# One hybrid decoder step: the small tile's own products cut in 32-column slices, meta updates over all 80 rows, and DeltaNet's sample keys and queries read as pairs

## The chip, the cores and the metric

The kernel runs on one NeuronCore of a Trainium2 chip. The metric is the time of the whole kernel on the device in microseconds (us), the median of several runs. One run was also recorded by the hardware profiler; rows called "the profile" or "the trace" come from that execution.

## The reference

One step of a decoder layer. A prompt of 1,024 tokens with 16 learned "meta" tokens in front, and 8 samples of 8 new tokens each, go through one input projection (2048 x 8984), three kinds of heads (6 mLSTM heads A, 6 gated-DeltaNet heads B, 4 HGRN2 heads C, each 128 wide), and an output projection (2048 x 2048). All values are 32-bit floats. For a prompt the state starts at zero and the 16 meta tokens are a chunk of their own; each sample starts from its own stored state.

```
# mLSTM, per chunk                    # gated DeltaNet, per chunk
num = a * (q @ C) + P @ v             W = U - Wk @ S
C_new = a_s * C + (w * k).T @ v       o = exp(G) * (q @ S) + Aqk @ W
n_new = a_s * n + sum(w * k)          S_new = exp(Ge) * S + (k * exp(Ge - G)).T @ W
# HGRN2, per chunk
o = (q * exp(b)) @ S + A @ v
S_new = exp(be) * S + (k * exp(be - b)).T @ v
```

So in each head every sample reads its own 128 x 128 state with its own 8 queries (DeltaNet with its 8 keys as well), while inside a sample, and among the 16 meta tokens, tokens see each other through a small masked matrix (P, Aqk, A).

## The kernel before, in words

The tokens are worked in two halves. Half 0 holds a **small tile** of 80 tokens (rows 0 to 63 are the 8 samples, 8 rows each; rows 64 to 79 are the meta tokens) and 512 prompt tokens in four tiles of 128. Half 1 holds the other 512 prompt tokens and no small tile. After both halves comes the output projection.

The bulk of the work on TensorE is the projection: a loop over weight pieces (`wraw`, loaded by SyncE's queue) that ScalarE and VectorE split into `whi` and `wlo`, multiplied with the tokens (`hA` in half 0, `hB` in half 1) into PSUM tiles `acc`. The heads' own work is written as generators and woven between these products: after each group of six `acc` products `weave.pump()` advances those head steps whose due time in a planner's clock has passed (each engine call adds a cost from a formula to that clock). The framework below may then move instructions on their engine. Every engine works through its own queue in order, so a TensorE product that waits holds back everything behind it there.

A 32-bit product stands in the trace as two instructions ("passes"). "128*32" in a row is rows times columns of TensorE's array that a product takes: rows are the partitions summed over, columns those of the result.

For the small tile in half 0 a head does this, and these are the places the change touches:

- `load_state` brings the 8 sample states of the head (512 KB) into `sst`, a single buffer.
- `sample_read` multiplies 8 samples' queries with their states: 8 products of 32 columns. Each sample's 8 columns stand in a zeroed block of 32 (`spread`), so that four samples add up in one group of 32 result rows and the read fills rows 0 to 63 of a PSUM tile: `nd` in A, `poh` in C, `po` in B. B calls it twice, for keys (`km`) and for queries (`qm`); the two `spread` tiles are used in turn by all heads.
- `small_rows` adds the tile's own products: one of 64 x 64 for the samples, one of 16 x 16 for the meta tokens.
- The meta tokens' state update is a product over the 16 meta rows alone (`pum` in A, `puh` in C, `pu` in B). In A a second product with `rowmask` over the 64 sample rows sums the keys for the normaliser `nsT`.
- In B, `side()` makes score matrices (`pqk`) and values (`pvb`) while VectorE inverts 16 x 16 blocks by substitution (`Yt`, `Yc` from coefficients `Bb` that went through memory); `px` transposes the result, and `first_chain` does the small tile's recurrence between the steps of the main tiles (`pz`, `pyy`, `px`).

Of the kernel before, what the change touches and what calls it, by code (L numbers as in the profile page):

```python
# [14 lines left out]
P = 128  # L15
# [165 lines left out]
def hybrid_step(ctx, tc, i, o):  # L181
# [353 lines left out]
    spread = [cp.tile([P, NB, 32], F32, name=f"spread{n}") for n in range(2)]  # L535
    spread_next = [0]
    for t in spread:
        G.memset(t, 0.0)

# [251 lines left out]
    def sample_read(st, src, dst, width, last=True):  # L791

        flat = src.rearrange("p b x -> p (b x)")
        for x in range(4):
            for j in range(2):
                b = 4 * j + x
                at_ = 32 * b - NS * x  # L800
                T.matmul(dst[32 * j:32 * (j + 1), 0:width], flat[:, at_:at_ + 32], st[:, b, 0:width],
                         start=x == 0, stop=last and x == 3)

    def small_rows(dst, rows, cols, width):

        for r in (slice(0, NSAMP), slice(NSAMP, NT0)):
            T.matmul(dst[r, 0:width], rows[r, r], cols[r, 0:width], start=r.start > 0, stop=True)
# [41 lines left out]
    def mlstm_scan(half, h, kT, qT, vT, tho, zs, nm, em, st):  # L849
# [52 lines left out]
        for g, kw, v1 in zip(half.groups, kws, v1s):  # L902
            if g.small:
                pu = bank("pum")
                T.matmul(pu[:, 0:P + 1], kw[NSAMP:NT0, 0], v1[NSAMP:NT0, 0], start=True, stop=True)
                T.matmul(pu[:, 2 * P:2 * P + NB], kw[0:NSAMP, 0], rowmask[0:NSAMP], start=True, stop=True)
                V.tensor_copy(Cn, pu[:, 0:P + 1])
                nsv = nsT.rearrange("p (b h) -> p b h", h=HA)[:, :, h:h + 1].rearrange("p b h -> p (b h)")
                nu = sp.tile([P, NB], F32, tag="nu", name="nu")
                V.tensor_tensor(nu, nsv, em[:, NS - 1:NSAMP:NS], op=ALU.mult)  # L910
                V.tensor_tensor(nsv, nu, pu[:, 2 * P:2 * P + NB], op=ALU.add)
                continue
# [16 lines left out]
        for g, E, kw, v1, og in zip(half.groups, Es, kws, v1s, ogs):  # L929
            n = g.n  # L930
            hx = gt("5", g)
            for c0 in range(0, g.nt, 2):
                cs = list(range(c0, min(c0 + 2, g.nt)))
                nd = bank("nd")
                for c in cs:
                    dst = nd[0:n, 256 * (c - c0):256 * (c - c0) + P + 1]
                    if g.small:
                        sample_read(st, qm, nd, P + 1, last=False)
                        small_rows(nd, E[:, c], v1[:, c], P + 1)
                        continue  # L940
                    T.matmul(dst, g.col(qd, c), Cn if c == 0 else Cs[:, c - 1], start=True, stop=False)
                    T.matmul(dst, E[0:n, c, 0:n], v1[0:n, c], start=False, stop=True)
# [80 lines left out]
    def gdn_scan(half, h, ck_, cq, cv, zs, Gb, eG, bb, st):  # L1023
# [70 lines left out]
        if half.first:  # L1094
            km, qm = spread_tile(), spread_tile()
            G.tensor_copy(km[:, :, 0:NS], sample_cols(knT))
            G.tensor_tensor(qm[:, :, 0:NS], sample_cols(cq), sample_cols(eG), op=ALU.mult)
# [31 lines left out]
        vbs, Aqs, kds = [], [], []  # L1129

        def side():
# [8 lines left out]
            yield  # L1140
            for g, kn in zip(gs, kns):
# [21 lines left out]
        def first_chain():  # L1163
            vb, Aq, kd, Y = vbs[0][:, 0], Aqs[0][:, 0], kds[0][:, 0], Ys[0][:, 0]
            po = bank("po0")
            sample_read(st, km, po, P)
# [8 lines left out]
            T.matmul(pu[:, 0:P], kd[NSAMP:NT0], W_[NSAMP:NT0], start=True, stop=True)  # L1175
            S.copy(Sm, pu[:, 0:P])
            po = bank("po1")
            sample_read(st, qm, po, P, last=False)
            small_rows(po, Aq, W_, P)
# [103 lines left out]
    def hgrn_scan(half, h, kT, lf, qT, vT, zs, st):  # L1283
# [90 lines left out]
        for g, v, kk in zip(gs, vs, kks):  # L1374
            pu = bank("puh")
            if g.small:
                T.matmul(pu[:, 0:P], kk[NSAMP:NT0, 0], v[NSAMP:NT0, 0], start=True, stop=True)
                V.tensor_copy(Sm, pu[:, 0:P])
                continue
# [10 lines left out]
        for g, v, kk in zip(gs, vs, kks):  # L1390
            n = g.n
            po = bank("poh")
            for c in range(g.nt):
                am = at0[0:n] if g.small else atv[:, c]
                dst = g.psum(po)[:, c]
                if g.small:
                    sample_read(st, qm, po, P, last=False)
                    small_rows(po, at0, v[:, 0], P)
                    continue
# [269 lines left out]
```

## Time and profile before

| | |
|---|---|
| median of 3 runs | 2603.36 us (2603.14 to 2606.81) |
| the profiled execution | 2607.68 us, span of its trace 2606.0 us |
| TensorE (PE) busy | 2549.4 us, 98% of the span |
| its weight loads (PEld), beside it | 2276.4 us, 87% |
| VectorE (DVE) | 1357.3 us, 52% |
| ScalarE (ACT) | 1005.8 us, 39% |
| GpSimd (POOL) | 533.6 us, 20% |
| memory | 121 GB/s over the span |

The profiled execution took 1.7 us more than its span. "Busy" joins instructions that overlap; a row of the timeline merges equal neighbours, so two products' lengths are compared by where rows start, not by the length printed. "[idle ... <- X]" at a row's end says how long the engine stood idle before it and what released it.

### The profile page before, as it was taken

The numbers are of one execution on the slowest core, as the hardware profiler recorded it, in microseconds if no ns is written. First come the engines' busy times: TensorE is split into PE (matmuls) and PEld (weight loads), VectorE is DVE, ScalarE is ACT, GpSimd is POOL, SyncE is SP. The second block draws the span as 40 slices with busy tenths as digits, with TensorE's granted clock in tenths as the row PEclk, the third lists the DMA queues.
The fourth block names the chain that finished last, engine by engine and source line by source line (L and its number), as shares of the span: only waits on it lengthen the run. The fifth ranks groups of instructions, "written<-read, shape, count | busy, mean of one in ns | idle before, by whom it ended". The sixth has DMA issues, their size and how long they took to land.

```text
span 2606.0 us, 43197 instructions
## 1 busy us (share of the span) xinstructions
PE 2549.4 (98%) x16160; PEld 2276.4 (87%) x16160; DVE 1357.3 (52%) x2811; ACT 1005.8 (39%) x2401; POOL 533.6 (20%) x656
## 2 busy tenths in 40 slices
PE   6899999999999999999999999999999999999998
PEld 5899999998999999999888888888888888888886
DVE  7664544654644654646674545455454545422435
ACT  5633334342334333324543434333433434322324
POOL 5221212321212321313230103111130102211201
PEclk9999999999999999999999999999999999999999
DMA  6633433555533433334644434343344437535735
GB/s 141 164 80 99 122 80 92 146 141 133 146 96 88 117 90 101 105 84 125 177 110 106 107 86 114 99 105 102 95 105 107 107 95 260 145 83 181 261 97 178
DMA packets 458461, 317.19 MB, mean 122 GB/s; under 512 B 56884, under 2 KB 402572, under 8 KB 457228
## 3 DMA queue, kind: packets, MB, share of 16 engines
q1 hardware_dynamic: 458252, 314.43, 44.6%
q8 instruction: 127, 2.08, 0.3%
q14 instruction: 82, 0.67, 0.1%
HBM read 268.93 MB, written 45.42 MB: 121 GB/s over the span
## 4 chain that ended last, share of the span: by engine, by line
PE 84%; issue 5%; DMA 4%; DVE 3%; POOL 2%; ACT 1%; SPq 1%; POOLq 0%; DVEq 0%; ACTq 0%
PE acc L127 60%; PE oacc L127 8%; PE pa L127 3%; PE po L127 1%; PE nd L127 1%; PE pu L127 1%; PE pz L127 1%; PE pyy L127 1%; POOL res L127 1%; PE poh L127 1%; DVE wlo L127 1%; POOL X L127 1%; PE pum L127 1%; PE py L127 1%; PE pw L127 0%
## 5 line engine op out<-in xcount | busy, mean ns | idle before, releaser
L127 PE MATMUL acc<-hA,whi 128*128 128x296 f32 x4544 | 837.8, 307 | 6.7 <-ACT whi L127 5.7
L127 DVE TENSOR_TENSOR wlo<-wraw,whi 128x512 fp32r<-128x512 f32 x720 | 520.9, 727 | 614.1 <-ACT whi L127 599.4
L127 ACT CAST whi<-wraw 128x512 fp32r<-128x512 f32 x720 | 443.3, 619 | 962.5 <-PE acc L127 667.0
L127 PE MATMUL acc<-hB,whi 128*128 128x512 f32 x2272 | 722.3, 400 | 0.0
L127 PEld LDWEIGHTS acc<-hA,whi 128*128 128x128 f32 x4544 | 683.1, 191 | 17.3 <-ACT whi L127 8.1
L127 PE MATMUL acc<-hA,wlo 128*128 128x296 f32 x2240 | 495.1, 301 | 5.3 <-DVE wlo L127 5.3
L127 PEld LDWEIGHTS acc<-hB,whi 128*128 128x128 f32 x2272 | 408.6, 188 | 76.6 <-issue 0.2
L127 PE MATMUL acc<-hB,wlo 128*128 128x512 f32 x1120 | 438.9, 392 | 1.2 <-DVE wlo L127 1.2
L127 PEld LDWEIGHTS acc<-hA,wlo 128*128 128x128 f32 x2240 | 368.0, 190 | 7.2 <-DVE wlo L127 6.9
L127 PE MATMUL oacc<-whi,y 128*128 128x512 f32 x1088 | 345.1, 392 | 1.4 <-ACT whi L127 1.4
L127 PEld LDWEIGHTS acc<-hB,wlo 128*128 128x128 f32 x1120 | 210.2, 188 | 48.9 <-DVE wlo L127 2.9
L127 PEld LDWEIGHTS oacc<-whi,y 128*128 128x128 f32 x1088 | 205.1, 189 | 45.1 <-ACT whi L127 2.7
L127 PE MATMUL oacc<-wlo,y 128*128 128x512 f32 x576 | 225.2, 391 | 0.7 <-DVE wlo L127 0.7
L127 PEld LDWEIGHTS oacc<-wlo,y 128*128 128x128 f32 x576 | 108.5, 188 | 23.8 <-DVE wlo L127 1.8
L127 POOL TENSOR_TENSOR res<-res,fnw 128x512 f32<-128x512 f32 (+1 forms) x34 | 54.3, 1623 | 259.1 <-ACT oscr L127 259.1
L127 POOL TENSOR_TENSOR qd<-qT,emb 128x512 f32<-128x512 f32 x12 | 15.9, 1326 | 359.1 <-PE po L127 287.2
L127 POOL TENSOR_TENSOR y<-y,zs 128x592 fp32r<-128x592 f32 (+1 forms) x32 | 45.9, 1434 | 140.3 <-ACT zs L127 130.1
L127 POOL TENSOR_TENSOR vx<-vh,rowmask 128x512 fp32r<-128x512 f32 x32 | 36.8, 1150 | 152.4 <-PE pu L127 79.5
L127 POOL TENSOR_TENSOR X<-Ex,hk 128x256 f32<-128x256 f32 (+2 forms) x40 | 37.4, 936 | 107.2 <-PE pa L127 93.0
L127 DVE TENSOR_TENSOR Yt<-Yc,Bb 128x60 f32<-128x60 f32 (+8 forms) x180 | 36.6, 203 | 43.7 <-DMA Bb<-db 38.6
L127 PE MATMUL pa<-X 128*128 128x128 f32 (+2 forms) x480 | 57.8, 260 | 0.0
L127 PEld LDWEIGHTS pa<-X 128*128 128x128 f32 (+2 forms) x480 | 50.0, 165 | 8.6 <-issue 0.9
(394 smaller groups left out, 2802.9 us busy)
## 6 DMA issues: line engine op xcount, KB each, us to landing
wraw<-in_w_in_dram SPq DMA_DIRECT2D x564, 256.0 KB
wraw<-in_w_out_dram SPq DMA_DIRECT2D x144, 256.0 KB
y<-y SPq DMA_DIRECT2D x16, 576.0 KB
px<-in_x_prompt_dram SPq DMA_DIRECT2D x32, 256.0 KB
out_dram<-sst SPq DMA_DIRECT2D x16, 512.0 KB
y<-zs SPq DMA_DIRECT2D x32, 256.0 KB
y<-y SPq DMA_DIRECT2D x32, 256.0 KB
res<-in_x_prompt_dram SPq DMA_DIRECT2D x32, 256.0 KB
```

The source lines that it names most:

```text
L127: return f(out, *a, **k)
```

## The change

Four edits, all of them in half 0.

1. `small_rows` is gone. `sample_read` adds the tile's own products itself, summed over all 80 rows, in slices of result rows 0 to 31, 32 to 63 and 64 to 79, each a product of at most 32 columns. The masked matrices are zero between one sample and another and between samples and meta tokens.
2. The meta update is summed over all 80 rows. Its right side is a copy of the values in one of two new tiles `metas`, whose first 64 rows are zero; ScalarE copies the 16 meta rows in (`meta_rows`). In A the columns behind the values hold `rowmask`, so that one product of 137 columns also gives the normaliser's sums.
3. In B the keys and queries of a sample stand side by side in one 32-column block (`pair_tile`, a third `spread` tile of its own). `sample_read_pair` reads all states once, 8 products of 32 columns into four groups of result rows, two samples to a group. It runs in the second step of `side()`; ScalarE copies the result to `rd`. Later two constant 0/1 matrices (`picks`) select from `rd` the key rows and the query rows, one full product each.
4. The third `spread` tile, `metas` and `picks` are filled once by GpSimd at the start.

```diff
-    def sample_read(st, src, dst, width, last=True):
+    def pair_tile():
+        return spread[2]
+
+    def sample_read(st, src, dst, width, rows, cols):
...
-                T.matmul(dst[32 * j:32 * (j + 1), 0:width], flat[:, at_:at_ + 32], st[:, b, 0:width],
-                         start=x == 0, stop=last and x == 3)
-
-    def small_rows(dst, rows, cols, width):
-
-        for r in (slice(0, NSAMP), slice(NSAMP, NT0)):
-            T.matmul(dst[r, 0:width], rows[r, r], cols[r, 0:width], start=r.start > 0, stop=True)
+                T.matmul(dst[32 * j:32 * (j + 1), 0:width], flat[:, at_:at_ + 32], st[:, b, 0:width], start=x == 0, stop=False)
+        for lo, hi, start in ((0, 32, False), (32, NSAMP, False), (NSAMP, NT0, True)):
+            T.matmul(dst[lo:hi, 0:width], rows[0:NT0, lo:hi], cols[0:NT0, 0:width], start=start, stop=True)
+
+    def sample_read_pair(st, src, dst):
+
+        flat = src.rearrange("p b x -> p (b x)")
+        for x in range(2):
+            for j in range(4):
+                b = 2 * j + x
+                at_ = 32 * b - 2 * NS * x
+                T.matmul(dst[32 * j:32 * (j + 1), 0:P], flat[:, at_:at_ + 32], st[:, b, 0:P], start=x == 0, stop=x == 1)
+
+    def meta_rows(src, width=P):
+
+        t = metas[metas_next[0] % 2]
+        metas_next[0] += 1
+        S.copy(t[NSAMP:NT0, 0:width], src[NSAMP:NT0, 0:width])
+        return t
...
-                T.matmul(pu[:, 0:P + 1], kw[NSAMP:NT0, 0], v1[NSAMP:NT0, 0], start=True, stop=True)
-                T.matmul(pu[:, 2 * P:2 * P + NB], kw[0:NSAMP, 0], rowmask[0:NSAMP], start=True, stop=True)
+                w = P + 1 + NB
+                T.matmul(pu[:, 0:w], kw[0:NT0, 0], meta_rows(v1[:, 0], P + 1)[0:NT0], start=True, stop=True)
...
         if half.first:
-            km, qm = spread_tile(), spread_tile()
-            G.tensor_copy(km[:, :, 0:NS], sample_cols(knT))
-            G.tensor_tensor(qm[:, :, 0:NS], sample_cols(cq), sample_cols(eG), op=ALU.mult)
+            kq = pair_tile()
+            G.tensor_copy(kq[:, :, 0:NS], sample_cols(knT))
+            G.tensor_tensor(kq[:, :, NS:2 * NS], sample_cols(cq), sample_cols(eG), op=ALU.mult)
...
             yield
+            if half.first:
+                pr = bank("pkq")
+                sample_read_pair(st, kq, pr)
+                rds.append(sq("rd", "rd", bufs=1))
+                S.copy(rds[0], pr[:, 0:P])
...
-            sample_read(st, km, po, P)
+            T.matmul(po[:NT0, 0:P], picks[0], rds[0], start=True, stop=True)
...
-            T.matmul(pu[:, 0:P], kd[NSAMP:NT0], W_[NSAMP:NT0], start=True, stop=True)
+            po = bank("po1")
+            T.matmul(po[:NT0, 0:P], picks[1], rds[0], start=True, stop=False)
+            T.matmul(po[:NT0, 0:P], Aq[:NT0, 0:NT0], W_[:NT0], start=False, stop=True)
+            T.matmul(pu[:, 0:P], kd[0:NT0], meta_rows(W_)[0:NT0, 0:P], start=True, stop=True)
             S.copy(Sm, pu[:, 0:P])
-            po = bank("po1")
-            sample_read(st, qm, po, P, last=False)
-            small_rows(po, Aq, W_, P)
...
-                T.matmul(pu[:, 0:P], kk[NSAMP:NT0, 0], v[NSAMP:NT0, 0], start=True, stop=True)
+                T.matmul(pu[:, 0:P], kk[0:NT0, 0], meta_rows(v[:, 0])[0:NT0, 0:P], start=True, stop=True)
```

Most of the order on the engines stays. On TensorE, in the first B head, this stood between the score products (`pqk`) and the transposed values (`pvb`) before:

```order
L127 MATMUL pqk<-Cq,knT 128x128 x4
L127 MATMUL acc<-hA_82,whi 128x296 x2
L127 MATMUL acc<-hA_83,whi 128x296 x2
L127 MATMUL acc<-hA_82,wlo 128x296 x2
...
L127 MATMUL pvb<-ident,Cv 80x128
L127 MATMUL pvb<-ident,Cv 128x128 x4
```

And this stands there now:

```order
L127 MATMUL pqk<-Cq,knT 128x128 x4
L127 MATMUL acc<-hA_82,whi 128x296 x2
L127 MATMUL acc<-hA_83,whi 128x296 x2
L127 MATMUL acc<-hA_82,wlo 128x296 x2
...
L127 MATMUL pkq<-sst,spread_714 32x128 x8
L127 MATMUL pvb<-ident,Cv 80x128
L127 MATMUL pvb<-ident,Cv 128x128 x4
```

The pair read of eight products is put in; the twelve `acc` products ahead of it are the same.

On ScalarE, in the first A head, the steps from the transposed values (`pv`) to the transposed output gate (`pot`) were these before:

```order
L127 COPY t_3314<-pv 80x128
L127 CAST kq<-kwall 64x128
L127 CAST vh<-t_3314 64x128 x2
L127 COPY s_3328<-pv 128x4x128
L127 CAST whi<-wraw 128x512
L127 ACTIVATE t_3373<-pot 80x128
```

Now they are these:

```order
L127 COPY t_3327<-pv 80x128
L127 CAST kq<-kwall 64x128
L127 COPY meta_715<-t_3327 16x129
L127 CAST vh<-t_3327 64x128 x2
L127 COPY s_3341<-pv 128x4x128
L127 CAST whi<-wraw 128x512
L127 ACTIVATE t_3386<-pot 80x128
```

The copy of the meta rows stands with the values' copies, ahead of the gate, though its call in the code comes after the gate.

On VectorE, at the end of the substitution of the third B head, the mask of the next B head (`bb`, a row that comes from memory) stood inside the substitution before:

```order
L127 TENSOR_TENSOR Yc<-Yc,Yt 128x5x3
L127 TENSOR_TENSOR bb<-bb,sm_642 80x80
L127 TENSOR_TENSOR Yt<-Yc,Bb 128x5x2
L127 TENSOR_TENSOR Yc<-Yc,Yt 128x5x2
L127 TENSOR_TENSOR wlo<-wraw,whi 128x512
L127 TENSOR_TENSOR Yt<-Yc,Bb 128x5
L127 TENSOR_TENSOR Yc<-Yc,Yt 128x5
L127 TENSOR_TENSOR t_7105<-Yc,submask 80x80
L127 TENSOR_TENSOR s_7107<-Yc,submask 128x512
```

Now it stands behind the substitution's result:

```order
L127 TENSOR_TENSOR wlo<-wraw,whi 128x512
L127 TENSOR_TENSOR Yc<-Yc,Yt 128x5x4
L127 TENSOR_TENSOR Yt<-Yc,Bb 128x5x3
L127 TENSOR_TENSOR Yc<-Yc,Yt 128x5x3
L127 TENSOR_TENSOR Yt<-Yc,Bb 128x5x2
L127 TENSOR_TENSOR Yc<-Yc,Yt 128x5x2
L127 TENSOR_TENSOR Yt<-Yc,Bb 128x5
L127 TENSOR_TENSOR Yc<-Yc,Yt 128x5
L127 TENSOR_TENSOR t_7116<-Yc,submask 80x80
L127 TENSOR_TENSOR s_7118<-Yc,submask 128x512
L127 TENSOR_TENSOR bb<-bb,sm_642 80x80
```

The mask and the row it needs are now waited for after the matrix that TensorE transposes next is done, and a split of weights (`wlo`) has moved by some places.

## Rows read from the trace of the kernel before

**Rows 1.** The page: busy time of the engines with its share of the span and the number of instructions, and the chain of work that ended last, by engine.

```profile
PE 2549.4 (98%) x16160; PEld 2276.4 (87%) x16160; DVE 1357.3 (52%) x2811; ACT 1005.8 (39%) x2401; POOL 533.6 (20%) x656
...
PE 84%; issue 5%; DMA 4%; DVE 3%; POOL 2%; ACT 1%; SPq 1%; POOLq 0%; DVEq 0%; ACTq 0%
```

**Rows 2.** Busy time in stretches of the span: from, to, length; then busy us (and instructions) of PE, PEld, DVE, ACT and POOL; the granted share of TensorE's clock; DMA share; GB/s. The first is the rest of half 0, the second half 1.

```profile
50.00:1290.00 1240.00, 1219.13 (x9342) 1173.12 (x9341) 688.95 (x1519) 482.05 (x1228) 288.51 (x378) 0.99 0.44 116
1290.00:2300.00 1010.00, 1008.80 (x5410) 839.30 (x5409) 512.21 (x1030) 399.28 (x920) 171.16 (x188) 1.00 0.43 115
```

**Rows 3.** Who waited for whom, whole core: us in total, times, longest us.

```profile
ACT whi L127 <- PE acc L127: 667.0, 346, 7.8
...
POOL spread L127 <- PE po L127: 109.5, 6, 28.9
...
PE pch L127 <- DMA cr<-in_state_gdn_conv_dram: 3.3, 1, 3.3
```

**Rows 4.** TensorE in the first A head, in order of time: start, length in us, instruction, rows*columns of the array, elements, count of passes.

```profile
289.25 0.71 PE L127 MATMUL pot<-ident,tho 128*80 128x128 f32 x5
289.89 0.48 PE L127 MATMUL pum<-t,kwall 16*128 16x129 f32 x2
290.30 0.39 PE L127 MATMUL pum<-rowmask,kwall 64*128 64x8 f32 x2
290.62 1.16 PE L127 MATMUL pum<-s,kwall 128*128 128x129 f32 x8
...
292.17 0.43 PE L127 MATMUL acc<-hA,wlo 128*128 128x296 f32 x2
...
293.34 1.08 PE L127 MATMUL nd<-sst,spread 128*32 128x129 f32 x16
294.35 0.75 PE L127 MATMUL nd<-t,t 64*64 64x129 f32 x4
295.03 0.81 PE L127 MATMUL acc<-hA,whi 128*128 128x296 f32 x4
295.69 0.43 PE L127 MATMUL acc<-hA,wlo 128*128 128x296 f32 x2
...
296.18 0.39 PE L127 MATMUL nd<-s,s 128*128 128x129 f32 x2
296.40 0.39 PE L127 MATMUL nd<-s,qd 128*128 128x129 f32 x2
```

**Rows 5.** TensorE at the transposed values of the first B head, the same columns.

```profile
211.19 0.43 PE L127 MATMUL acc<-hA,wlo 128*128 128x296 f32 x2
211.46 0.71 PE L127 MATMUL pvb<-ident,Cv 128*80 128x128 f32 x5
...
212.56 0.43 PE L127 MATMUL acc<-hA,wlo 128*128 128x296 f32 x2
```

**Rows 6.** TensorE at the state update of the first C head, the same columns.

```profile
166.69 0.44 PE L127 MATMUL acc<-hA,wlo 128*128 128x296 f32 x2
167.06 0.48 PE L127 MATMUL puh<-t,t 16*128 16x128 f32 x2
...
169.03 0.44 PE L127 MATMUL acc<-hA,wlo 128*128 128x296 f32 x2
```

**Rows 7.** TensorE in the first chain of the first B head, the same columns.

```profile
231.31 1.05 PE L127 MATMUL pz<-s,Ball 128*128 128x128 f32 x8
232.29 1.07 PE L127 MATMUL po<-sst,spread 128*32 128x128 f32 x16
233.29 0.81 PE L127 MATMUL acc<-hA,whi 128*128 128x296 f32 x4
233.95 0.43 PE L127 MATMUL acc<-hA,wlo 128*128 128x296 f32 x2
...
236.97 0.60 PE L127 MATMUL px<-ident,s 128*128 128x128 f32 x4
237.50 0.48 PE L127 MATMUL pu<-Wt,t 16*128 16x128 f32 x2
237.91 1.07 PE L127 MATMUL po<-sst,spread 128*32 128x128 f32 x16
238.92 0.75 PE L127 MATMUL po<-Wt,t 64*64 64x128 f32 x4
...
240.25 0.44 PE L127 MATMUL acc<-hA,wlo 128*128 128x296 f32 x2
```

**Rows 8.** ScalarE's copy of the small tile's values in the first A head; start, length.

```profile
284.78 0.26 ACT L127 COPY t<-pv 80x128 f32<-80x128 f32 x1 [0.68 <-PE pv L127]
```

**Rows 9.** The first B head's sample keys on GpSimd, and its state's load where SyncE's queue issues it; start, length.

```profile
202.96 0.64 POOL L127 COPY spread<-knT 128x64 f32<-128x64 f32 x1
...
194.41 0.37 SPq L811 DMA_DIRECT2D sst<-in_state_gdn_S_dram  x1
```

**Rows 10.** GpSimd's first statistic at the start; start, length, idle time before it.

```profile
10.09 0.55 POOL L127 TENSOR_TENSOR xss<-xss,halfneg 80x1 f32<-80x1 f32 x1 [3.51 <-DVE xss L127]
```

**Rows 11.** The end of the substitution in the third B head: VectorE's mask of the next head, and TensorE's transposes of the result.

```profile
608.70 0.24 DVE L127 TENSOR_TENSOR bb<-bb,sm 80x80 f32<-80x80 f32 x1 [1.42 <-DMA bb<-rows]
...
611.59 1.09 PE L127 MATMUL px<-ident,s 128*128 128x128 f32 x4 [4.76 <-DVE s L127]
```

**Rows 12.** The tile `nd`: TensorE's loads of the left side in the sample reads, count, ns of one (least, median, most), first and last start in us.

```profile
L127 PEld LDWEIGHTS nd<-sst,spread x96: 106/110/113, 293.3 to 1202.3; 128*32 128x32 f32 x96
```

More of the change, by code (lines that the diff above doesn't have):

```diff
@@ L534, in hybrid_step @@
         G.affine_select(v, v, pattern=[[NS, NB]], compare_op=ALU.is_ge, fill=0.0, base=NS - 1, channel_multiplier=-1)
-    spread = [cp.tile([P, NB, 32], F32, name=f"spread{n}") for n in range(2)]
+    spread = [cp.tile([P, NB, 32], F32, name=f"spread{n}") for n in range(3)]
     spread_next = [0]
-    for t in spread:
+    metas = [cp.tile([P, P + 1 + NB], F32, name=f"meta{n}") for n in range(2)]
+    metas_next = [0]
+    for t in spread + metas:
         G.memset(t, 0.0)
+    for t in metas:
+        G.tensor_copy(t[0:NSAMP, P + 1:], rowmask[0:NSAMP])
+    picks = [cp.tile([P, NT0], F32, name=f"pick{n}") for n in range(2)]
+    for n, t in enumerate(picks):
+        G.memset(t, 0.0)
+        G.tensor_copy(t[:, 0:NSAMP].rearrange("p (b x) -> p b x", x=NS),
+                      ident.rearrange("p (b x) -> p b x", x=2 * NS)[:, :, NS * n:NS * (n + 1)])
     state_A = [cp.tile([P, P + 1], F32, name=f"state_A{h}") for h in range(HA)]
@@ L910, in mlstm_scan @@
                 V.tensor_tensor(nu, nsv, em[:, NS - 1:NSAMP:NS], op=ALU.mult)
-                V.tensor_tensor(nsv, nu, pu[:, 2 * P:2 * P + NB], op=ALU.add)
+                V.tensor_tensor(nsv, nu, pu[:, P + 1:w], op=ALU.add)
                 continue
@@ L937, in mlstm_scan @@
                     if g.small:
-                        sample_read(st, qm, nd, P + 1, last=False)
-                        small_rows(nd, E[:, c], v1[:, c], P + 1)
+                        sample_read(st, qm, nd, P + 1, E[:, c], v1[:, c])
                         continue
@@ L1127, in substitute @@
                 Ys.append(Y)
-        vbs, Aqs, kds = [], [], []
+        vbs, Aqs, kds, rds = [], [], [], []
         def side():
@@ L1396, in hgrn_scan @@
                 if g.small:
-                    sample_read(st, qm, po, P, last=False)
-                    small_rows(po, at0, v[:, 0], P)
+                    sample_read(st, qm, po, P, at0, v[:, 0])
                     continue
```

## The prediction, made before the changed kernel ran

> **What bounds the kernel now.** I read the page's busy times first. TensorE is busy for 98% of the span and makes up 84% of the chain that ended last [rows 1]. A share over the whole span can hide a stage with another limit, so the table by stretches came next: in the rest of half 0, the only part that the change touches, TensorE is busy for 1219 of 1240 us at a granted clock of 0.99 of full speed (nearly all of it at the upper of its two levels, 2.4 GHz), while VectorE has 689, ScalarE 482 and GpSimd 289 [rows 2]. Then the waits: ScalarE's split of weights waited 667 us in all for TensorE to give back buffers [rows 3], so the split weights lie ready and TensorE uses them up. Time taken from TensorE's queue in half 0 is therefore time taken from the span, until something else is late. What is left is to price the small tile's products, and that can't be done from their printed lengths, since neighbours overlap. I use starts alone.
>
> **Two measures.** Full products follow each other at 0.22 us, two passes of 0.11 (296.18 to 296.40) [rows 4]. A run of full products that goes over into the four `acc` passes without another array shape between needs 0.11 a pass and then 0.55: the five transposes start at 211.46 and the `wlo` pair behind the `acc` passes at 212.56, which is 1.10 = 5 x 0.11 + 0.55 [rows 5]. The pair ahead takes 0.27 (211.19 to 211.46). With these I build what each place takes after the change, and subtract it from what the rows show.
>
> **Meta update in A.** From `pot` at 289.25 to `wlo` at 292.17 are 2.92 us [rows 4]. Two short products go (16 and 64 rows), with two more array shapes between full ones; one full product of 137 columns comes, 0.22 x 137/128 = 0.24. After: 5 x 0.11 + 0.24 + 4 x 0.22 + 0.55 = 2.22. Saved: 0.70.
>
> **Meta update in C.** From `wlo` at 166.69 to the next at 169.03 are 2.34 us [rows 6]. After: 0.27 + 5 x 0.22 + 0.55 = 1.92. Saved: 0.42 in three heads. In the fourth no `acc` product lies ahead and the update follows right on the keys' copies on ScalarE, where the new copy is queued too; I count nothing there.
>
> **Own products in A and C.** From the read at 293.34 to `wlo` at 295.69 are 2.35 us: 16 read passes, the 64 x 64 and the 16 x 16 product, then `acc` [rows 4]. The same read with `acc` right behind it is in B: 232.29 to 233.95, 1.66 [rows 7]. The three slices have the read's 32-column shape, so only their own time is added. The read runs two column groups side by side: 16 passes in 1.01 us (293.34 to 294.35, one change of shape included), which is eight rounds. Three slices in three groups are two rounds of 0.11 if three groups go side by side too, 0.66 if one by one. I take 0.22, as nearest to the read's rows. After: 1.88; saved 0.47 (0.03 at the other end). The section "Part 3: Packing small matmuls" of the Trainium skill's page "TensorE: Matmul & The Clock Gate" gives three column tiles as 2.38 times as fast as one by one. By that the slices would take 0.66/2.38 = 0.28 and the sum below would be 0.6 us less; no row here has three groups.
>
> **First chain in B.** The key read: from `pz` at 231.31 to `wlo` at 233.95, 2.64 us; with one full product instead, 8 x 0.11 + 0.22 + 0.55 = 1.65. Saved: 0.99. So a read between full products costs 2.64 - 8 x 0.11 - 0.55 = 1.21 with both changes of shape. The query read with the meta update and own products: from `px` at 236.97 to `wlo` at 240.25, 3.28 us; after the change these are four transposes and three full products, 4 x 0.11 + 3 x 0.22 + 0.55 = 1.65. Saved: 1.63 [rows 7].
>
> **The pair read in B** is new between `acc` and `pvb`. It has four groups of 32 columns and two samples in each: four rounds instead of eight, 1.21 - 4 x 0.11 = 0.77. If only two groups go side by side it costs the full 1.21; one by one, 16 x 0.11 + 0.33 = 2.09 (0.33 is what the read's 1.21 has over its eight rounds). I take 0.77, since each of the read's rounds holds whatever groups stand next to each other.
>
> **Sum on TensorE:** A, 6 x (0.70 + 0.47) = 7.0; C, 3 x 0.42 + 4 x 0.47 = 3.1; B, 6 x (0.99 + 1.63 - 0.77) = 11.1. Together 21.2 us.
>
> **What is added elsewhere, and what hides it.** ScalarE gets 22 copies; the nearest one takes 0.26 [rows 8], so 6 us in the stretch in which it idles for 758. In A the copy stands right behind the values' copy, done at about 285.6, and `pum` starts at 289.89: 4 us of cover. Without it TensorE would stand for the copy, 0.26 us a head and the way there and back. The pair read needs the keys on GpSimd, done at 203.60 [rows 9], 7.9 us ahead of `pvb` [rows 5], and the state. Its load is issued at 194.41 [rows 9] and was read at 232.29; now it is read at about 211.5, 17 us after its issue. At the 116 GB/s of this stretch [rows 2] 512 KB take 4.5 us. GpSimd gains: its writes of the next `spread` waited 109.5 us for B's reads [rows 3], and these now end a chain step or two earlier. That releases the states' decay sooner and with it their way out to memory; nothing on the chain hangs on it. The new tiles are filled at the start by nine short instructions, in the 3.51 us that GpSimd waits for the first statistic [rows 10]. None is larger than the copy of 0.64 [rows 9]; at that bound they take 5.8, and 2.3 us would be added to the start once. I take them at half of it and so at nothing.
>
> **One stall moves.** In the third B head TensorE stood 4.76 us at `px` for VectorE, and VectorE had stood 1.42 us inside the substitution for the next head's mask row, and worked 0.24 on it [rows 11]. In the new order the mask stands behind the substitution. That takes 1.66 from VectorE, and the pair read's 0.77, already charged, now fills part of the stall: 2.4 us back, between 0 (the coefficients themselves come later) and all 4.76. What may be late instead: at one place `pch` waited 3.3 us for a small load that SyncE's queue issued just before [rows 3], and the order of loads shifts a little there. I charge half of it, 1.6, as a new wait.
>
> **Result.** 21.2 + 2.4 - 1.6 = 22.0 us. The profiled execution would have a span of 2606.0 - 22.0 = 2584.0 and take 2585.7. It lies 4.3 above the median of the runs, 2603.36; taken from that, I predict **2581 us**. A measurement of this kernel tells about 0.2% (5.2 us) from no change.
>
> **The rivals.**
>
> - *Column groups go one by one* (chance 6%). The slices then save 0.03 instead of 0.47 and the pair read costs 2.09: 22.0 - 10 x 0.44 - 6 x 1.32 = 9.7 us, 2594. Against it: a load of the left side takes 110 ns [rows 12], 16 of them would be 1.76 us, and the whole read took 1.01 [rows 4], so loads run beside each other and beside passes. The same section of the Trainium skill says that a weight load overlaps running products only where the row group differs; here all groups use all rows, so by that rule this rival would be the outcome. The trace's two groups speak against the rule.
> - *Two at a time* (chance 12%, within my range). The pair read costs 1.21 and the slices 0.44: 22.0 - 6 x 0.44 - 10 x 0.22 = 17.2, 2586.
> - *Slower: the early pair read waits for its state* (chance 5%). It stands in TensorE's queue with all weight products behind it. SyncE issues the load behind the write of the head before from the same single buffer. Six waits of more than 22.0/6 = 3.7 us turn the change into a loss; the load would have to land over 17 + 3.7 = 21 us after its issue. Waits of 5 us in each head give 2603.4 - 22.0 + 30 = 2611. Against it: the 4.5 us above.
> - *No change: the time comes back as waiting* (chance 6%). Weights or VectorE's splits would have to be the true limit in half 0, and the freed time would stand as idle time before `acc`; 2600 to 2606. Against it: ScalarE's 667 us of waiting for TensorE [rows 3], and 0.44 of the DMA time used in that stretch [rows 2].
> - *Partly eaten* (chance 8%): shifted steps make two or three stalls like the one of 4.76 us; 2587 to 2597.
>
> **How the numbers follow.** The rest, 63%, is the forecast: 2576 to 2586, from all of the 4.76 back and no new wait (2577), to nothing back and a new wait of 3.3 (2585.5), with 1 us for how runs differ. The range 2574 to 2592 goes below it by the other wait of before, the 3.3 at `pch`, which may go instead of come (2577.4 - 3.3), and above it over the two-at-a-time case and most of the partly eaten one. It leaves out some 18%. Faster by over 0.2%: the forecast, both cases of column groups and the partly eaten one, 89%. Within 0.2%: 6%. Slower: 5%.
>
> **What would show it.** Right: in the changed trace `pum` of 80*128 starts about 0.11 a pass behind `pot`, with no 16*128, 64*64 or 16*16 shapes in the heads; from `nd` read to the `wlo` behind it about 1.88; the six pair reads take about 0.5 each, with 0.77 more between `acc` and the `wlo` behind `pvb`; TensorE's busy time falls by about 20 us, its idle time hardly changes; half 1 is as long as before. Wrong: the passes of `pkq` start one by one, 0.11 apart; idle time stands before `pkq` released by the state's DMA or by GpSimd; `pum`, `puh` or `pu` wait for the meta copy; or new idle time before `acc`, `px` or `pch` adds up to more than 5 us.

## The result and the profile after

The changed kernel takes 2582.9 us (median of four runs, 2581.8 to 2583.7) against 2605.1 for the kernel before, measured beside it: 22.2 us less, a ratio of 0.9911 with a 95% interval of 0.9897 to 0.9925. The forecast was 2581, 22.0 us less; it was taken from a median of 2603.4 before, and 1.7 of the 1.9 us between 2581 and 2582.9 are that difference. The profiled execution has a span of 2581.6 us where 2584.0 was forecast.

The page of the changed kernel, busy times and the chain, which answer to [rows 1]:

```profile
PE 2525.8 (98%) x16084; PEld 2264.0 (88%) x16084; DVE 1352.9 (52%) x2811; ACT 1010.8 (39%) x2423; POOL 534.9 (21%) x665
...
PE 82%; issue 5%; DMA 5%; DVE 3%; POOL 2%; ACT 1%; SPq 1%; POOLq 0%; DVEq 0%; ACTq 0%
```

TensorE is still the bound. It is busy for 23.6 us less, and ScalarE for 5.0 more: the 22 copies that were counted at nothing. The stretches of the changed kernel, with the columns of [rows 2]; I set the bound between them 20 us earlier:

```profile
50.00:1270.00 1220.00, 1198.08 (x9278) 1163.09 (x9278) 686.71 (x1522) 490.06 (x1253) 289.14 (x378) 0.99 0.45 118
1270.00:2280.00 1010.00, 1009.19 (x5412) 839.64 (x5411) 510.46 (x1028) 396.95 (x918) 170.38 (x187) 1.00 0.43 115
```

Half 1 then has the same work as there (5412 instructions on TensorE, 5410 there) in the same 1010 us, so it gains nothing, as was said. By the start of the same pass, the 8000th of TensorE's `acc` passes in half 1, the changed kernel is 23.0 us ahead (1598.6 before, 1575.6 now), and about 1.5 of the 24.4 us between the two spans come in the last 36 us, where the change edits nothing. Filling the new tiles cost nothing: the first `acc` pass starts at 31.5 in both. Now the places. TensorE in the first A head of the changed kernel answers to [rows 4]: start, length, instruction, rows*columns of the array, elements, count of passes.

```profile
287.13 0.71 PE L127 MATMUL pot<-ident,tho 128*80 128x128 f32 x5
287.68 0.40 PE L127 MATMUL pum<-meta,kwall 80*128 80x137 f32 x2
...
289.35 0.43 PE L127 MATMUL acc<-hA,wlo 128*128 128x296 f32 x2
...
290.54 0.97 PE L127 MATMUL nd<-sst,spread 128*32 128x129 f32 x14
291.24 0.28 PE L127 MATMUL nd<-t,t 80*16 80x129 f32 x1
291.34 0.28 PE L127 MATMUL nd<-sst,spread 128*32 128x129 f32 x2
291.36 0.48 PE L127 MATMUL nd<-t,t 80*16 80x129 f32 x5
...
292.41 0.43 PE L127 MATMUL acc<-hA,wlo 128*128 128x296 f32 x2
```

From `pot` to `wlo` are now 2.22 us, to the hundredth what was worked out, and from the read to `wlo` 1.87 (1.88 was forecast). The slices cost the two rounds that were charged. The one of 16 columns even starts at 291.24, ahead of the read's last two passes; the read does not use its column group.

TensorE in the first B head, where the new pair read stands, answers to [rows 5]; the same columns.

```profile
211.02 0.43 PE L127 MATMUL acc<-hA,wlo 128*128 128x296 f32 x2
211.38 0.65 PE L127 MATMUL pkq<-sst,spread 128*32 128x128 f32 x16
211.96 0.75 PE L127 MATMUL pvb<-ident,Cv 128*80 128x128 f32 x5
...
213.08 0.43 PE L127 MATMUL acc<-hA,wlo 128*128 128x296 f32 x2
```

From `wlo` to `wlo` it is 2.06 us, where [rows 5] have 212.56 - 211.19 = 1.37. The pair read costs 0.69; 0.77 was charged.

TensorE in the first chain of the same head answers to [rows 7]; the same columns.

```profile
231.80 1.05 PE L127 MATMUL pz<-s,Ball 128*128 128x128 f32 x8
232.69 0.38 PE L127 MATMUL po<-rd,pick 128*80 128x128 f32 x2
...
233.45 0.44 PE L127 MATMUL acc<-hA,wlo 128*128 128x296 f32 x2
...
237.30 0.60 PE L127 MATMUL px<-ident,s 128*128 128x128 f32 x4
237.73 0.38 PE L127 MATMUL po<-rd,pick 128*80 128x128 f32 x2
237.95 0.38 PE L127 MATMUL po<-Wt,t 80*80 80x128 f32 x2
238.17 0.39 PE L127 MATMUL pu<-meta,t 80*128 80x128 f32 x2
...
238.94 0.43 PE L127 MATMUL acc<-hA,wlo 128*128 128x296 f32 x2
```

1.65 and 1.64 us; 1.65 was forecast for both. Then TensorE's waits, which answer to [rows 3] and [rows 11]: us in all, times, longest.

```profile
PE px L127 <- DVE bb L127: 4.1, 1, 4.1
...
PE pch L127 <- DMA cr<-in_state_gdn_conv_dram: 1.8, 1, 1.8
PE pw L127 <- DVE s L127: 1.5, 1, 1.5
...
PE puh L127 <- ACT meta L127: 1.1, 1, 1.1
```

This is the part that did not come as forecast. `px` still waits for VectorE, 4.09 us instead of 4.76; the wait at `pch` became shorter, not longer; and the waits at `pw` and, for the meta copy, at `puh` are new. VectorE at the end of the third B head's substitution shows why. The columns are start, length, instruction, count, and idle time ahead with what ended it.

```profile
592.07 0.20 DVE L127 TENSOR_TENSOR Yc<-Yc,Yt 128x40 f32<-128x40 f32 x1
594.26 0.75 DVE L127 SCALAR_TENSOR_TENSOR px<-px,bss,pnw 128x512 f32<-128x512 f32 x1 [1.99 <-DMA px<-in_x_prompt_dram]
594.93 0.18 DVE L127 TENSOR_TENSOR Yt<-Yc,Bb 128x35 f32<-128x35 f32 x1
...
599.01 0.68 DVE L127 TENSOR_TENSOR s<-Yc,submask 128x512 f32<-128x512 f32 x1
599.61 0.23 DVE L127 TENSOR_TENSOR bb<-bb,sm 80x80 f32<-80x80 f32 x1
```

The mask row `bb` did move behind the substitution. But the norm of a prompt tile for half 1 (also named `px`, in `prep_B`) moved into it, waits 1.99 us for its load and works 0.75: 2.7 us in the place of 1.66. In the kernel before it stood behind `s<-Yc`.

### The profile page after: what moved, and what is told of

The parts are those of the page before. It is cut to its first block, busy times and chain, and to the rows that moved or that the text cites. A ratio compares the mean times of both kernels' runs of the same rounds, so it can differ in the third digit from the quotient of the medians.

```text
span 2581.6 us, 43090 instructions
## 1 busy us (share of the span) xinstructions
PE 2525.8 (98%) x16084; PEld 2264.0 (88%) x16084; DVE 1352.9 (52%) x2811; ACT 1010.8 (39%) x2423; POOL 534.9 (21%) x665
## 3 DMA queue, kind: packets, MB, share of 16 engines
q8 instruction: 126, 2.06, 0.3%
## 4 chain that ended last, share of the span: by engine, by line
PE 82%; issue 5%; DMA 5%; DVE 3%; POOL 2%; ACT 1%; SPq 1%; POOLq 0%; DVEq 0%; ACTq 0%
PE acc L127 60%; PE oacc L127 8%; PE pa L127 2%; PE pu L127 1%; PE po L127 1%; PE pz L127 1%; PE pyy L127 1%; DMA wraw<-in_w_in_dram 1%; PE nd L127 1%; DMA wraw<-in_w_out_dram 1%; POOL res L127 1%; PE poh L127 1%; POOL X L127 1%; DVE wlo L127 1%; DMA px<-in_x_prompt_dram 1%
## 5 line engine op out<-in xcount | busy, mean ns | idle before, releaser
L127 PEld LDWEIGHTS oacc<-wlo,y 128*128 128x128 f32 x576 | 108.2, 188 | 24.5 <-DVE wlo L127 2.5
```

The source lines that it names most:

```text
L127: return f(out, *a, **k)
```

## The experiments

My theory: TensorE's time at each place adds up to 21 to 22 us, and that is the gain; where VectorE's small operations and the small loads fall is a second effect that can be several us either way. The rival: the gain came from stalls that moved.

**The parts one by one.** The slices of the A and C heads alone:

```
-                        sample_read(st, qm, nd, P + 1, last=False)
-                        small_rows(nd, E[:, c], v1[:, c], P + 1)
+                        sample_slices(st, qm, nd, P + 1, E[:, c], v1[:, c])
...
```

> The kernel before with one part of the change alone: the small tile's own products of the A and C heads in 32-column slices. Theory (the gain is TensorE's time at each place, and it adds up): the stretch from the acc pass ahead of a read to the first wlo pass behind it falls from 2.57 to about 2.11 us in A and from 2.55 to 2.10 in C, all else stays, so 10 x 0.46 = 4.6 us less: ratio about 0.998. Rival (most of the change's gain is stalls that moved with the order): the stretch falls too, but the total moves by something else, between 0.9965 and 1.001, and idle time of TensorE changes by more than 2 us.

Measured: 2596.7 us, ratio 0.9972 (0.9961 to 0.9983), 7.7 us less by the medians; the interval, 4.4 to 10.2 us, holds the 4.6 that was expected. The stretches fell as expected, to 2.11 in A and 2.10 in C. Stalls moved as well: `px` waits at two places (2.94 and 2.42 us) and `pch` not at all.

The meta updates of the A and C heads alone:

```
-                T.matmul(pu[:, 0:P + 1], kw[NSAMP:NT0, 0], v1[NSAMP:NT0, 0], start=True, stop=True)
-                T.matmul(pu[:, 2 * P:2 * P + NB], kw[0:NSAMP, 0], rowmask[0:NSAMP], start=True, stop=True)
+                T.matmul(pu[:, 0:w], kw[0:NT0, 0], meta_rows(v1[:, 0], P + 1)[0:NT0], start=True, stop=True)
...
```

> The kernel before with one part alone: the meta updates of the A and C heads as one product over all 80 rows, with the copy of the meta rows on ScalarE; the B heads are left as before. Theory (places add up): from the acc pass ahead of pot to the wlo pass behind pum 3.05 falls to 2.35 us in four to six A heads, puh's stretch from 2.20 to 1.80 in three C heads; the fourth C head waits about 0.8 us longer at puh for the new copy and gains at most 0.4 there: 6 x 0.70 + 3 x 0.40 - 0.4 = 5.0 us less, ratio about 0.998. Rival (moved stalls): a total between 0.9965 and 1.001 with TensorE's idle time changed by more than 2 us.

> The meta updates alone once more, for its trace. By the places: 6 x 0.70 + 3 x 0.40 - 0.4 = 5.0 us of TensorE's time less. Measured before: 3.1 us less than the kernel before. Theory: the places show the 5.0, and the rest is in longer stalls at px, pw, pch or acc. Rival: the places show less than 5.0.

Measured: ratios 0.9990 (0.9980 to 0.9999) and 0.9986 (0.9977 to 0.9996), 3.1 us less by the medians in either; both intervals (0.3 to 5.2 and 1.0 to 6.0 us) hold the 5.0. The trace, that of the second, has 2.36 in four A heads (in the other two no `acc` pass follows `pum` directly), 1.80 in three C heads and the longer wait at `puh`, so the 5.0 us are at their places.

The DeltaNet part alone is the changed kernel with both edits above taken back; what is left against the kernel before, in part:

```
+                sample_read_pair(st, kq, pr)
...
-            sample_read(st, km, po, P)
+            T.matmul(po[:NT0, 0:P], picks[0], rds[0], start=True, stop=True)
```

> The kernel before with the DeltaNet part alone: keys and queries read as pairs, picks in the first chain, its meta update over 80 rows; A and C heads as before. Theory (places add up): the key read's stretch falls from 2.78 to 1.79, the query read's from 3.42 to 1.78, and 0.70 comes back ahead of pvb: 6 x 1.93 = 11.6 us less, ratio 0.9955. The mask row bb stands inside the third B head's substitution as before, so px there should stand for about 4.8 us as before. Rival (moved stalls): the gain is 5 us or more off from that.

Measured: 2583.9 us, ratio 0.9921 (0.9906 to 0.9936), 20.5 us less where 11.6 was expected, which lies outside the interval (16.7 to 24.5). The places have 1.79, 1.78 and 1.93 in each head, just as in the whole change, so 9 us came from elsewhere: `px` waits 1.03 us (4.76 in the kernel before) and `pch` 0.27 (3.25). The mask row does stand inside the substitution and waits there; but TensorE's `acc` passes ahead of `px` last until 602.6, and VectorE's `s<-Yc` starts at 602.8, where it was 606.8 and 610.8 in the kernel before.

By the totals alone one would say that the slices and meta updates are worth nothing beside the DeltaNet part (2583.9 and 2582.9). So neither theory holds alone: the places add up, and stalls of up to 9 us come and go with the order.

**What makes `px` late: the tiles' buffers.** SyncE's queue waited long for one thing that concerns half 1 only, the writes of normed prompt tiles, whose buffers the next loads need. The waits of SyncE's queue in the changed kernel (it is 20.0 us in the kernel before):

```profile
SPq L563 <- DMA hbhi<-px: 18.2, 12, 3.2
```

And the queue itself at the stall of the changed kernel: the writes of the last tile, and the next load.

```profile
585.53 0.63 SPq L599 DMA_DIRECT2D hblo<-hblo  x1
...
590.76 0.35 SPq L563 DMA_DIRECT2D px<-in_x_prompt_dram  x1
```

The edit, at three places with this tag:

```
-            x = sp.tile([P, 512], F32, tag="px", name="px", bufs=3)
+            x = sp.tile([P, 512], F32, tag="px", name="px", bufs=4)
```

> The changed kernel with four buffers in place of three for the prompt tiles that are normed ahead for half 1 (tag px). Theory (VectorE's norm of a prompt tile stands in the middle of the third B head's substitution and waits 1.99 us for a load that SyncE can issue only when a buffer is free): with the load issued earlier the 1.99 us go, px's stall of 4.09 falls to 2 or less, and the 1.46 us at pw for the next such load go: 3 to 6 us less than the changed kernel (the passes behind a long stall run at a lower granted clock, which gives some of it), ratio to before about 0.9895. Rival (the load is late because the DMA engines are busy, or it is another buffer that is late): the stall stays at about 4 us and the ratio at 0.991.

Measured: 2572.35 us, ratio 0.9879 (0.9863 to 0.9896), 10.5 us less than the changed kernel where 3 to 6 were expected. This version is the fastest of all. SyncE's queue in it:

```profile
582.72 0.62 SPq L599 DMA_DIRECT2D hblo<-hblo  x1
583.39 0.65 SPq L563 DMA_DIRECT2D px<-in_x_prompt_dram  x1
```

The load goes out 0.67 us behind the write instead of 5.2, and the wait for buffers is gone from the queue's list. `px` waits 2.25 us, `pw` not at all, `pch` 0.75. The three waits are 4.3 us shorter in sum (3.0 against 7.3). Behind two of them the granted clock of the changed kernel is 0.66 for 5 us and 0.83 for 10, a loss of 1.7 each; here it is 1.00 in both places. That is 7.7 of the 10.5. By the starts of the same `acc` passes the rest lies in three pieces of about 1 us: at the start of half 0, where the `acc` and `pc` waits are shorter too, between the 2400th and the 2800th pass, and at the end of half 0.

> The kernel before with one edit: four buffers in place of three for the prompt tiles of half 1 (tag px). Theory A (TensorE's products are worth 21.5 us at their places, and what three buffers do to SyncE's queue, which stood 20 us for writes of these tiles with other loads behind it, is a separate matter in either kernel): this kernel loses the long stalls at px and pch too and gains 6 to 10 us, to 2595 to 2599; the changed kernel with four buffers lies 21 to 24 us under it. Rival B (the stalls of the kernel before have other causes, its px stall the mask row's load and its pch stall its own small load): it gains less than 3 us, and four buffers are worth 10 us only in the changed kernel, whose order puts a norm into the substitution.

Measured: 2595.9 us, ratio 0.9970 (0.9958 to 0.9982). Theory A holds in its totals: this kernel has the same trouble, and gains 9 us by the same edit. `px` waits 0.45 us there; `pch` still waits 2.19, so that stall did not go as expected. The changed kernel with four buffers lies 23.6 us under it.

> The DeltaNet part alone, with four buffers for the prompt tiles. Theory A (the A and C parts save 9.9 us of TensorE's time whatever the stalls do; with three buffers they were eaten because the order shifts and px, pw and pch wait): with four buffers the DeltaNet part alone has little to gain, 0 to 3 us (2581 to 2584), and the whole change with four buffers lies 8 to 11 us under it. Rival B (the A and C parts are worth little beside the pair read): it gains about 10 us as the whole change does, to about 2573.

Measured: 2580.8 us, ratio 0.9909 (0.9894 to 0.9925): 3 us from four buffers, and the whole change lies 8.5 us under it. The A and C parts do have their worth (9.9 us by the places); with three buffers stalls ate it. The DeltaNet part alone lies 15.1 us under the kernel before, both with four buffers, 3.5 more than its places: `pch` waits 0.93 us there instead of 2.19 and `pw` 0.51 instead of 1.44, and the granted clock is 1.00 behind `pch`, where it was 0.66 from 694 to 699.

> The changed kernel with four buffers for the prompt tiles and two in place of one for their scratch and norm weights (tag pxs), for which SyncE's queue stood 6.4 us. Theory (every wait in SyncE's queue delays the loads behind it): less than the changed kernel with four buffers by 0 to 3 us. Rival (that wait stands where nothing behind it is late): no difference from it, 2572.

On top of the four buffers, at both places with this tag:

```
-            scr = sp.tile([P, 512], F32, tag="pxs", name="pxs", bufs=1)
+            scr = sp.tile([P, 512], F32, tag="pxs", name="pxs", bufs=2)
```

Measured: 2577.0 us, ratio 0.9896 (0.9879 to 0.9912), not faster but 4.7 us slower than with four buffers alone (the intervals overlap from 0.9879 to 0.9896, the times themselves do not: 2575.7 to 2578.8 against 2571.5 to 2573.7). My theory missed. 2.9 us of it lie at the start of half 0, where the same `acc` passes, the 201st to the 401st, take 33.9 us (75.5 to 109.4) against 31.0 (76.0 to 107.0). The changed kernel with three buffers, where `pxs` has one, takes 33.7 for them too, with a wait of 3.44 us at the same pass; why that wait is back with a second scratch buffer stays open. From 95 to 125 TensorE's idle time here is 5.6 us, one wait of 3.17 in it; in the other kernel it is 6.5 us, parts of seven waits, the longest 1.82. The same stretch, first of this kernel, then of the one with four buffers alone (columns of [rows 2]):

```profile
95.00:125.00 30.00, 24.42 (x140) 23.30 (x139) 19.20 (x48) 17.49 (x41) 10.59 (x12) 0.79 0.57 154
```

```profile
95.00:125.00 30.00, 23.48 (x160) 21.70 (x161) 21.93 (x52) 18.08 (x44) 10.28 (x12) 1.00 0.59 153
```

The first is busy for longer and does less in it (140 instructions against 160), because its granted clock is 0.79 of full speed.

**What makes `px` late: the order.** With four buffers `px` still waited 2.25 us. The planner puts the norm a given time behind its load; I changed that number.

```
-            ck.last = ck.t["T"] + 6.0
+            ck.last = ck.t["T"] + 7.0
```

> The changed kernel with four buffers for the prompt tiles, and the planner told to put their norm 7.0 instead of 6.0 us behind; by that neither a norm nor the mask row stands in the third B head's substitution. Theory (what VectorE does and waits for inside the substitution is what px stands for): px's stall falls from 2.25 us to under 1, the total lies 0 to 3 us under the changed kernel with four buffers (2569 to 2573). Rival (the coefficients' own load or the substitution itself is late): px's stall stays at about 2.

> The changed kernel with three buffers as it has them, and the planner's 7.0 in place of 6.0: the norm moves out of the third B head's substitution, the waits of SyncE's queue for the prompt tiles' buffers stay. Theory (the norm inside cost 2.7 us of px's 4.09, and the queue's waits make other loads late): px's stall falls to about 1.4, pch or pw still wait 1 to 3 us, total 2576 to 2581, between the changed kernel and the one with four buffers. Rival (buffers alone matter): px's stall stays at about 4 and the total at 2583; or (order alone matters): 2572.

Measured: with four buffers 2579.1 us, ratio 0.9911 (0.9896 to 0.9925), against the expectation slower than without the edit; with three buffers 2576.9, ratio 0.9904 (0.9887 to 0.9921), as expected. What decides is seen on VectorE. With four buffers and 7.0:

```profile
593.52 0.17 DVE L127 TENSOR_TENSOR Yc<-Yc,Yt 128x5 f32<-128x5 f32 x1
596.12 0.75 DVE L127 SCALAR_TENSOR_TENSOR px<-px,bss,pnw 128x512 f32<-128x512 f32 x1 [2.44 <-DMA px<-in_x_prompt_dram]
...
596.94 0.69 DVE L127 TENSOR_TENSOR s<-Yc,submask 128x512 f32<-128x512 f32 x1
```

With three buffers and 7.0:

```profile
592.91 0.17 DVE L127 TENSOR_TENSOR Yc<-Yc,Yt 128x5 f32<-128x5 f32 x1
...
593.27 0.68 DVE L127 TENSOR_TENSOR s<-Yc,submask 128x512 f32<-128x512 f32 x1
593.90 0.75 DVE L127 SCALAR_TENSOR_TENSOR px<-px,bss,pnw 128x512 f32<-128x512 f32 x1
```

In the first the norm left the substitution but stands ahead of the masking copy that `px` waits for; I had looked only at the substitution. In the second it stands one row later. TensorE at `px`, first with four buffers and 7.0, then with three:

```profile
597.78 0.63 PE L127 MATMUL px<-ident,s 128*128 128x128 f32 x4 [2.91 <-DVE s L127]
```

```profile
596.65 0.60 PE L127 MATMUL px<-ident,s 128*128 128x128 f32 x4
```

It waits 2.91 us in the first and not at all in the second, where 1.4 was expected. The two kernels differ in buffers as well, so it is the rows that show the cause: in the first VectorE stands 2.44 us for the norm's load right ahead of the copy, in the second it does the copy before the norm. What four buffers are worth is not the same at every order (10.5 us, 8.9, 3.1, and with 7.0 a loss of 2 that lies inside the intervals); why `pch` and `pu` wait longer in the kernel with 7.0 and four buffers was not followed up.

**The prices on TensorE.**

```
-        for x in range(2):
-            for j in range(4):
+        for j in range(4):
+            for x in range(2):
...
-                T.matmul(pu[:, 0:w], kw[0:NT0, 0], meta_rows(v1[:, 0], P + 1)[0:NT0], start=True, stop=True)
+                T.matmul(pu[:, 0:P + 1], kw[0:NT0, 0], mv[0:NT0, 0:P + 1], start=True, stop=True)
+                T.matmul(pu[:, P + 1:w], kw[0:NT0, 0], mv[0:NT0, P + 1:w], start=True, stop=True)
```

> The changed kernel with two edits that are read at their own places. (1) The pair read's loops exchanged: the two products of a column group follow each other, then come the next group's. From the acc pass ahead of pkq to the first wlo pass behind pvb the changed kernel takes 1.93 us. Theory A (each column group works off its own products, whatever stands between them in the code): four starts side by side in each of four rounds, 1.93 as before. Rival B (only neighbours in the code run side by side): the passes of a group hold up those of the next, some 13 rounds in place of 4, 2.9 us. (2) The A heads' meta update as two products of 129 and 8 columns over the same 80 rows. Stretch now 2.35, in the kernel before 3.05. Theory A (most of the 0.70 was two changes of array shape): 2.57 at most, two passes of 0.11 more. Rival B (it was the number of products): 3.05.

Measured at the places: the pair read's stretch 1.96 us with the loops exchanged, and the meta update's 2.57 (four of `pum`'s passes where there were two), the last at the four A heads where `acc` stands on both sides. Theory A for both. So of the 0.70 saved, the second product itself was 0.22; the rest, 0.48, went with the 16-row and 64-row shapes. (The total, 2584.5 us, is one run and no price.)

```
-                T.matmul(dst[32 * j:32 * (j + 1), 0:P], flat[:, at_:at_ + 32], st[:, b, 0:P], start=x == 0, stop=x == 1)
+                T.matmul(dst[0:32, 0:P], flat[:, at_:at_ + 32], st[:, b, 0:P], start=b == 0, stop=b == 7)
...
+                T.matmul(pr[:, 0:P], ident, st[:, 0, 0:P], start=True, stop=True)
```

> The changed kernel with the pair read's eight products all sent to the first column group, behind one full product of 128 columns that fills the other rows; the values it leaves for the B heads' small tile are therefore not the reference's. Theory (the four groups run side by side in the changed kernel and one group takes its passes one by one): 16 rounds in place of 4 and a full product, 12 x 0.11 + 0.22 = 1.5 us more at each of six places, 1.93 becomes 3.5. Rival (loads of the left side set the pace in either case): 1.93 becomes 2.2.

TensorE there:

```profile
212.48 0.38 PE L127 MATMUL pkq<-sst,ident 128*128 128x128 f32 x2
212.79 1.94 PE L127 MATMUL pkq<-sst,spread 128*32 128x128 f32 x16
214.66 0.74 PE L127 MATMUL pvb<-ident,Cv 128*80 128x128 f32 x5
```

The stretch is 3.44 us: from the first of the 16 passes to `pvb` it is 1.87 us one by one (212.79 to 214.66), and 0.58 in four groups (211.38 to 211.96). The total (2586.6, one run) is only 4 us over the changed kernel, not 9, since `px` waits 0.61 us in this order; it is not a price.

## Why the prediction was right, and where it was not

- **TensorE's terms.** 21.2 us were forecast. The rows give 6 x (0.70 + 0.48) + 3 x 0.40 + 4 x 0.45 + 6 x (0.99 + 1.64 - 0.69) = 21.7. No term is off by more than 0.1 a head. (The A and C terms are read where `acc` stands on both sides, in four A heads and three C heads. Of the others, the fifth A head, where the same products follow each other, gives 0.69 and 0.46.) Counting starts between neighbours and pricing by 0.11 a pass and 0.55 for the `acc` passes carried over to every place.
- **The rivals on column groups** fall: four side by side, 1.93 and 1.96 in the two orders, 3.44 in one group. The rule of the Trainium skill ("TensorE: Matmul & The Clock Gate", "Part 3: Packing small matmuls") that a weight load overlaps only where the row group differs is not what these traces show, where all groups use the same rows: the 16 loads of the first pair read, 106 to 110 ns each, all start within 0.27 us.
- **The early pair read** waits for nothing: no wait at `pkq` stands in TensorE's list. That rival falls, in this kernel.
- **The meta copies** are hidden in A and in three C heads. The fourth C head got its new wait: no weight pass lies there to cover the copy. ScalarE and TensorE there:

```profile
1252.09 0.59 ACT L127 COPY s<-pkh 128x512 f32<-128x512 f32 x1
1252.70 0.29 ACT L127 COPY meta<-t 16x128 f32<-16x128 f32 x1
```

```profile
1253.05 0.49 PE L127 MATMUL puh<-meta,t 80*128 80x128 f32 x2 [1.09 <-ACT meta L127]
```

The wait was 0.29 and is 1.09. From the first `pkh` pass to the read it is 3.11 us (1251.25 to 1254.36), where it was 2.57 (1274.57 to 1277.14): a loss of 0.5 us, where I counted nothing.
- **The moved stall** is the step that failed. I gave 2.4 us: 1.66 for the mask row's going and 0.77 for the pair read, which would fill part of the stall. The row went, and another operation came: the wait is 0.7 us shorter, not 2.4. The order of the changed kernel showed that too (the excerpt ahead begins behind the norm's new place); I had searched it for the row that I knew, not for all that stands between the substitution's first operation and `px`.
- **The new wait** of 1.6 us charged at `pch` had the wrong sign: it fell from 3.25 to 1.77. New were `pw` (1.46) and `puh` instead.
- **A wait that I did not name** gave the most: an `acc` pass waited 2.88 us for `wlo` at 492 in the kernel before, and 1.60 at the same pass now. Behind the first the granted clock is 0.67 from 492 to 497, behind the second 1.00 from 484 to 494. From the 2400th to the 2600th `acc` pass it is 2.7 us less.
- **The price of a stall** was too low. I counted idle time alone. The stretches from the start of `px`'s stall on, first of the kernel before, then of the changed one (columns of [rows 2]):

```profile
606.00:612.00 6.00, 1.24 (x9) 1.02 (x8) 4.27 (x15) 0.62 (x1) 0.70 (x1) 0.81 0.63 147
612.00:618.00 6.00, 6.00 (x41) 5.68 (x39) 2.15 (x5) 0.59 (x1) 0.00 (x0) 0.62 0.44 119
618.00:624.00 6.00, 6.00 (x57) 5.51 (x55) 4.31 (x7) 3.36 (x9) 1.43 (x2) 1.00 0.40 122
```

```profile
595.00:600.00 5.00, 0.91 (x8) 0.69 (x7) 4.55 (x21) 0.32 (x1) 0.74 (x1) 1.00 0.28 80
600.00:605.00 5.00, 5.00 (x30) 5.00 (x30) 2.64 (x5) 1.17 (x2) 0.00 (x0) 0.66 0.59 151
605.00:610.00 5.00, 5.00 (x42) 5.00 (x41) 2.80 (x6) 2.48 (x7) 1.14 (x2) 1.00 0.57 167
```

Behind the stall the granted clock is 0.62 for 6 us, so 6 x 0.38 = 2.3 us are lost on top of the 4.76; in the changed kernel 5 x 0.34 = 1.7 on top of 4.09. All of the stall was worth 7 us, more than the upper end of 4.76 that I gave it; the kernel before with four buffers, where `px` waits 0.45 us, takes 6.6 us less from the 3100th to the 3400th `acc` pass.

The stalls together were forecast at +0.8 us. They came out near that (22.2 in all less 21.7 by the medians; 24.4 less 21.7 between the two profiled executions), but by terms of other sizes and signs that happened to cancel: 2.7 us at `wlo`, 2.2 at `pch` and, with its clock, 1.3 at `px` came back, 1.9 went at `pw` and 0.7 at the start of half 0, and the rest lies in smaller waits. The three parts alone sum to 31 us, the whole gives 22. The forecast's middle owes that to luck; its TensorE terms don't.

## What to carry to other kernels

On an engine that is busy throughout, price an edit by starts between neighbours at each place; such terms add up, and a change of array shape can be worth more than the product. Then list everything that the order puts ahead of the one instruction that the busy engine waits for, down to the last copy, and what each waits for: here one norm of the next half, one row earlier or later, made 3 us and more of difference. Don't judge parts of a change by totals alone while such stalls are there; take their cause away first (here one more buffer) and compare then.

## What the chip showed that I had not expected

- Products sent to four column groups run side by side whichever stands next in the code: with each group's two products behind each other the 16 passes still start four at a time (stretch 1.96 us against 1.93), and a slice for a free group starts ahead of products that stand before it in the code (291.24 and 291.34 above). "In order", as the description ahead has it, holds here within a column group.
- A wait can cost TensorE more than its length. Behind idle times of 4.76 and 4.09 us the granted clock was 0.62 and 0.66, and around the one of 3.17 it was 0.79 over 30 us; with seven shorter waits that sum to more it was 1.00, and the work went through 2.9 us sooner. After the 2.25 us at `px` with four buffers it stayed at 1.00. But around the 1.77 us at `pch` in the changed kernel it was 0.83 from 690 to 700, and around the 2.19 us there in the kernel before with four buffers 0.66 from 694 to 699, so the length of the last wait alone does not tell it.
- A product whose right side has 8 columns costs as much as one with 128: two passes, 0.22 us (2.57 against 2.35).
